# First product of a two-block kernel: input transposed without its norm, row factors applied to values, queries and keys

## The chip, the cores and the metric

One core of a Trainium2 chip runs the whole program. The metric is the device time of one execution in microseconds (us), the median of several runs. The trace is of one profiled execution.

## The reference, cut to what matters

Two transformer-like blocks on `x`, 256 rows of 1024, in fp32. The part at issue is the first layer of the first block:

```python
def rmsnorm(x, g):
    xf = x.astype(jnp.float32)
    y = xf * lax.rsqrt(jnp.mean(xf * xf, axis=-1, keepdims=True) + RMS_EPS)
    return (y * g.astype(jnp.float32)).astype(x.dtype)

hn = rmsnorm(h, norm_mix[layer])
# in chunked_band_attention(hn, ...), 16 heads of 64:
qkv = jnp.einsum('bsd,de->bse', h, w_qkv)
s = jnp.einsum('bqhd,bkhd->bhqk', q_c, k_band) * scale + bias
p = jax.nn.softmax(s, axis=-1)
o = jnp.einsum('bhqk,bkhd->bqhd', p, v_band)
```

After it come an output product, a squared-ReLU MLP, a gated recurrent layer with its MLP, and a second block with two SwiGLU products, windowed attention and pooling. The norm is a factor r for each row of x and a gain g for each of its 1024 features. A product of the normed row is r times the product of the row with its gains alone.

## The kernel before

**Numbers in two parts.** Every large product is made of three fp32r products: each operand is split into a high part (ACT copies it to fp32r) and a low part (DVE subtracts the high part), and TensorE adds high x high, low x high and high x low. Weights come from HBM in pieces of 128 x 1024 (512 KB) into four `raw` buffers, are split into `wh` (10 buffers) and `wl` (7 buffers), and a `raw` buffer is free again when its low part is made. `Core.load` and `Core.fetch` issue the DMAs on SP's queue, in the order of `c.plan`; `weights` asks for three pieces ahead.

**Order of the work.** TensorE runs its instructions in the order in which the program writes them. On the other engines a scheduler orders instructions by priority and readiness; `urgent()` raises the priority of a block, and `issue_after(ins)` keeps the instructions of a block behind `ins` on the engine that they share with it. Each engine then runs its queue in order.

**The start (`forward`).** The tiles `h[0]` and `h[1]` hold 128 rows of x each; `fetch(t)` loads one in two halves. `spread` loads the gain row of 1024 and, by two 1-row products with a column of ones, writes it to all 128 partitions in PSUM (line 230). `stat` squares a half row with its sum on ACT (line 488), `sum` adds the sums and the epsilon on DVE (497), `power` takes the power -1/2 on POOL (506), and `finish` multiplies h by r and by the gains on DVE into `hn` (512). `turned` transposes hn in eight blocks of 128 x 128 per tile on TensorE (527), and `split` makes from each four of them the two parts of `xt` (ACT line 109, DVE line 113). Tile 1 follows in the same way while the first product runs.

**The values (`a_gen`, name `v`).** The stationary operand is a block of xt, the moving one 512 columns of a weight. With `head=5` the first five of eight contraction blocks k are done for tile 0 and then for tile 1 (the high products of block k are written before the low ones of k-1); the transposes of tile 1 stand between the steps (`mid`). Then follow the rest, and the last three blocks per bank (`tail=3`), after which `evac_v` copies each bank to `vt`. 96 products of 512 columns in all, at lines 381 and 385 (a_v in the trace).

**Queries and keys (`b_gen`).** Four rounds of a query piece and a key piece, each of two blocks of 128 features. The weight is stationary, xt moves: the high parts with 512 columns (line 249), the low with 256 (258). `evac` calls `join`, which adds the two parts of a product: ACT copies one (337), DVE adds it to the other (341 for keys, 343 for queries, with the scale 1/8). During a round the attention of the heads of the round before is woven in: `scores` (734), softmax, `turn` (765), `apply` (776). `decay`, some thirty operations on 128 x 8 numbers for the recurrent layer, is written after the first round; its input `cols`, and for the second block `rope` and `sink`, are small DMAs on SP's queue.

Of the kernel before, what the change touches and what calls it, by code (L numbers as in the profile page):

```python
# [9 lines left out]
F32 = mybir.dt.float32  # L10
F32R = mybir.dt.float32r
AF = mybir.ActivationFunctionType
ALU = mybir.AluOpType
# [35 lines left out]
def run(gen):  # L49
    for _ in gen:  # L50
        pass
# [14 lines left out]
def rest():  # L66
    pass


class Core:  # L70
# [146 lines left out]
            self.nc.sync.dma_start(t, self.a["rows"][row : row + 1, :].to_broadcast([P, D]))  # L217
        return [t[:, n * 512 : (n + 1) * 512] for n in range(2)]

    def spread(self, row, name):  # L220

        nc = self.nc
        one = self.const.tile([1, P], F32, name="one")
        nc.vector.memset(one, 1.0)
        t = self.gb.tile([P, D], F32, tag="gb", name=f"row_{name}")
        nc.sync.dma_start(t[0:1, :], self.a["rows"][row : row + 1, :])
        out = []
        for n in range(2):
            out.append(self.psum(f"{name}_{n}"))
            nc.tensor.matmul(out[n], one, t[0:1, n * 512 : (n + 1) * 512], start=True, stop=True)  # L230
        return out

    def b_gen(self, xt, blocks, evac, fill=0, mid=(), late=(3, 4), whole=None):
# [129 lines left out]

        return lhs

    def a_gen(self, name, nk, lhs, evac, head=0, mid=(), tail=4, hook=(), late=0, half=False):


        nc = self.nc
        acc = {}

        def bank(t, n):
            if (t, n) not in acc:
                acc[t, n] = self.psum(f"a_{name}_{t}{n}")
            return acc[t, n]

        def high(k, t, n, part):
            w = self.weights(name, k)[:, n * 512 : (n + 1) * 512]  # L380
            nc.tensor.matmul(bank(t, n), lhs(k, t, part), w, start=k == 0 and not part, stop=False)  # L381

        def low(k, t, n):
            w = self.weights(name, k, True)[:, n * 512 : (n + 1) * 512]
            nc.tensor.matmul(bank(t, n), lhs(k, t, 0), w, start=False, stop=k == nk - 1)  # L385

        def mm(k, t, n):
            high(k, t, n, 0)
            high(k, t, n, 1)
            low(k, t, n)  # L390

        mid, hook = list(mid), list(hook)
        for t in range(2 if head else 0):
            for k in range(head):
                for part in range(2):
                    for n in range(2):
                        high(k, t, n, part)
                for n in range(2 if k else 0):
                    low(k - 1, t, n)
                if t == 0 and k >= head - 2 and mid:  # L400
                    mid.pop(0)()
                yield
            for n in range(2):
                low(head - 1, t, n)
        for f in mid:
            f()
        for k in range(head, nk - tail):
            for t in range(2):
                for n in range(2):
                    mm(k, t, n)  # L410
                yield
        normed = bool(hook)
        if normed:
            self.approach(name, nk - 1)
        for t in range(2):
            for n in range(2):
                for i, k in enumerate(range(nk - tail, nk)):
                    mm(k, t, n)
# [30 lines left out]
class Norm:  # L449


    def __init__(self, c, row, name, scale=None, spread=False):
        self.c, self.name, self.scale = c, name, scale
        self.g = (c.spread if spread else c.gain)(row, f"g_{name}")
        self.sums, self.hn = {}, {}
        self.x = None

# [59 lines left out]
    def turned(self, t):  # L517


        def half(n):  # L520
            c = self.c
            if self.x is None:

                self.x = c.xt.tile([P, KD, 2, 2, P], F32R, tag="xt", name=f"xt_{self.name}")
            ps = c.psum(f"tr_{self.name}{t}_{n}")
            for i in range(4):
                c.nc.tensor.transpose(
                    ps[:, i * P : (i + 1) * P], self.hn[t][:, n * 512 + i * P : n * 512 + (i + 1) * P],
                    c.ident,
                )  # L530
            k = slice(4 * n, 4 * n + 4)
            with c.urgent():
                c.turned = c.split(
                    self.x[:, k, t, 0, :], self.x[:, k, t, 1, :], ps.rearrange("p (k n) -> p k n", n=P)
                )

        return [lambda: half(0), lambda: half(1)]


class Norm2(Norm):  # L540
# [88 lines left out]
@with_exitstack  # L629
def forward(ctx: ExitStack, tc, a, out):  # L630
    nc = tc.nc
    c = Core(ctx, tc, a)
    ctx.enter_context(tc.manual_schedule(engines={mybir.EngineType.PE}))

    def fetch(t):
        for n in range(2):
            cc = slice(n * 512, (n + 1) * 512)
            nc.sync.dma_start(c.h[t][:, cc], a["x"][0, t * P : (t + 1) * P, cc])

    norm = Norm(c, R_MIX0, "mix0", spread=True)  # L640
    fetch(0)
    c.planned("v", a["w_v"])
    with c.urgent():
        for n in range(2):
            norm.stat(0, n)
        norm.finish(0)
    c.hold = True
    c.load(1)
    for i, f in enumerate(norm.turned(0)):
        f()  # L650
        with c.behind():
            if not i:
                c.lows()
            else:
                c.hold = False
            c.load(2 + i)
            if not i:
                fetch(1)
    with c.urgent(), c.behind():
        for n in range(2):  # L660
            norm.stat(1, n)
        norm.finish(1)
# [36 lines left out]

def attention(c, norm, cols):  # L700
# [3 lines left out]
    vt = c.slot("vt")  # L704

    def evac_v(t, n, ps, cc):
        nc.scalar.activation(vt[:, t * D + n * 512 : t * D + (n + 1) * 512], ps, AF.Copy)

    run(c.a_gen(
        "v", KD, lambda k, t, s: xt[:, k, t, s, :], evac_v, head=5, mid=norm.turned(1), tail=3,  # L710
    ))

    qt, kt, ot = c.slot("qt"), c.slot("kt"), c.slot("ot")
    bias = [c.slot(f"bias{i}") for i in range(2)]
# [3 lines left out]

    def evac(name, f, ps):
        dst = blk(qt if name[0] == "q" else kt, f)  # L720
        c.join(
            dst.rearrange("p (t n) -> p t n", n=P), ps, f"{name}_{f}", scale=0.125 if name[0] == "q" else 1.0
        )

    state = {}

# [69 lines left out]
    for j in range(4):  # L796
        gen = c.b_gen(xt, [(f"q{j}", 0, 2 * j), (f"k{j}", 0, 2 * j)], evac)
        weave(gen, 8, pairs(2 * j - 2, 2 * j) if j else [])
        if not j:
            nc.sync.dma_start(cols, a["cols"])  # L800
            decay(c, cols)
    norm = Norm(c, R_MLP0, "mlp0")
    gen = c.a_gen(
        "ao", KD, c.stationary("ao", lambda i: ot[:, i * 512 : (i + 1) * 512]), norm.evac,
# [163 lines left out]
def mixer(c, norm, cols):  # L968
    nc, a = c.nc, c.a
    xt = norm.x  # L970
    rope = c.const.tile([P, 2, 2, 16], F32, name="rope")
    nc.sync.dma_start(rope, a["rope"])
    sink = c.const.tile([P, 8], F32, name="sink")
    nc.sync.dma_start(sink, a["sink"][0:1, :].to_broadcast([P, 8]))
    less = c.const.tile([P, 8], F32, name="less")
    nc.vector.tensor_scalar_mul(less, sink, -1.0)
    pm, pools, mix, ro, rot = (c.slot(f"mix{i}") for i in range(5))
# [337 lines left out]
```

## Time and profile before

| | us |
|---|---|
| median of 3 runs (lowest, highest) | 1009.74 (1009.57, 1010.5) |
| the profiled execution | 1008.66 |
| its span in the trace | 1006.9 |
| TensorE busy | 994.7 (99%) |
| VectorE (DVE) busy | 665.7 (66%) |
| ScalarE (ACT) busy | 573.7 (57%) |
| GpSimd (POOL) busy | 28.8 (3%) |

The profile follows each instruction of every engine. PE is TensorE's products, PEld the loading of their stationary operands, which overlaps them, SP the queue that issues most DMAs. Ends of products are modelled, since they are pipelined: the step from one start to the next is the better measure of their rate. `[0.62 <-DVE kt L341]` behind a row says that the engine had been idle for 0.62 us and what ended that. A row in order of time merges neighbours (`x8`). Most fp32 products (not fp32r) appear as two records. Lines are those of the kernel before.

### The profile page before, as it was taken

What the parts mean: (1) busy time and instruction counts of PE and PEld (TensorE: products, weight loads), DVE (VectorE), ACT (ScalarE), POOL (GpSimd) and SP (SyncE); (2) the same over time, 40 slices, a digit from 0 to 9 for tenths busy, and PEclk for the clock granted to TensorE, in tenths of its full rate; (3) what the DMA queues carried; (4) which work ended last, traced back from release to release, by engine and by line L of the source; (5) the groups of instructions that cost most, each with busy time, mean ns of one, the idle gap of its engine ahead of it and who ended that gap; (6) DMA issues with size and microseconds to landing.
All of it is one profiled execution on the core that took longest, in us unless ns stands there. A gap on an engine that the chain in (4) does not pass through costs nothing.

```text
span 1006.9 us, 14600 instructions
## 1 busy us (share of the span) xinstructions
PE 994.7 (99%) x5558; PEld 856.5 (85%) x5558; DVE 665.7 (66%) x1070; ACT 573.7 (57%) x950; POOL 28.8 (3%) x49
## 2 busy tenths in 40 slices
PE   8999999999999999999999999999999999999997
PEld 6887898888889989888888988888888698888885
DVE  6677487676648768867555876565557767756553
ACT  6576556455537965654544665555436856555541
POOL 1000000000012200000000000000000000000000
PEclk9999999999999999999999999999999999999999
DMA  8944157667744454767653476676526428566641
GB/s 279 328 149 132 58 185 254 209 229 231 256 141 131 142 168 147 252 201 239 203 191 126 156 246 190 196 252 213 182 70 224 147 65 268 193 196 203 208 143 42
DMA packets 52055, 187.41 MB, mean 186 GB/s; under 512 B 6161, under 2 KB 6161, under 8 KB 51474
## 3 DMA queue, kind: packets, MB, share of 16 engines
q1 hardware_dynamic: 51986, 186.49, 56.8%
q8 instruction: 43, 0.70, 0.3%
q14 instruction: 26, 0.21, 0.1%
HBM read 185.42 MB, written 1.05 MB: 185 GB/s over the span
## 4 chain that ended last, share of the span: by engine, by line
PE 89%; ACT 4%; DMA 3%; DVE 2%; issue 1%; POOLq 0%; POOL 0%; SPq 0%; ACTq 0%; DVEq 0%
PE b_m L249 12%; PE a_n L381 11%; PE a_d L381 8%; PE b_g L249 8%; PE b_u L249 8%; PE b_m L258 6%; PE a_n L385 6%; PE b_g L258 4%; PE b_u L258 4%; PE a_d L385 4%; PE b_r L270 2%; PE a_v L381 2%; PE a_ao L381 1%; PE a_ro L381 1%; PE a_mo L381 1%; PE b_r L249 1%
## 5 line engine op out<-in xcount | busy, mean ns | idle before, releaser
L381 PE MATMUL a_n<-wh_n,l_n 128*128 128x512 f32 x512 | 157.9, 390 | 0.0
L249 PE MATMUL b_m<-xt_mlp,wh_m 128*128 128x512 f32 (+1 forms) x608 | 124.8, 357 | 0.0
L249 PEld LDWEIGHTS b_m<-xt_mlp,wh_m 128*128 128x128 f32 x608 | 100.6, 189 | 14.9
L381 PEld LDWEIGHTS a_n<-wh_n,l_n 128*128 128x128 f32 x512 | 95.7, 188 | 19.5
L113 DVE TENSOR_TENSOR wl_n<-raw_n,wh_n 128x1024 fp32r<-128x1024 f32 x64 | 78.1, 1223 | 51.5 <-PE a_n L385 38.8
L134 ACT ACTIVATE wh_n<-raw_n 128x1024 fp32r<-128x1024 f32 x64 | 67.9, 1061 | 76.2 <-DMA raw_n<-in_w_m_dram 75.3
L381 PE MATMUL a_d<-wh_d,l_d 128*128 128x512 f32 x352 | 108.7, 390 | 0.0
L385 PE MATMUL a_n<-wl_n,l_n 128*128 128x512 f32 x256 | 99.6, 389 | 0.0
L113 DVE TENSOR_TENSOR wl_m<-raw_m,wh_m 128x1024 fp32r<-128x1024 f32 x64 | 77.3, 1221 | 24.7 <-PE b_m L258 17.3
L134 ACT ACTIVATE wh_m<-raw_m 128x1024 fp32r<-128x1024 f32 x64 | 67.4, 1058 | 44.3 <-DMA raw_m<-in_w_m_dram 44.1
L249 PE MATMUL b_g<-xt_ffn,wh_g 128*128 128x512 f32 (+1 forms) x416 | 86.5, 359 | 0.2 <-ACT wh_g L134 0.2
L249 PE MATMUL b_u<-xt_ffn,wh_u 128*128 128x512 f32 (+1 forms) x384 | 85.0, 373 | 0.0
L249 PEld LDWEIGHTS b_g<-xt_ffn,wh_g 128*128 128x128 f32 x416 | 69.2, 189 | 11.2 <-ACT wh_g L134 0.4
L381 PEld LDWEIGHTS a_d<-wh_d,l_d 128*128 128x128 f32 x352 | 65.8, 188 | 13.5
L113 DVE TENSOR_TENSOR wl_d<-raw_d,wh_d 128x1024 fp32r<-128x1024 f32 x44 | 53.6, 1223 | 35.2 <-PE a_d L385 23.6
L249 PEld LDWEIGHTS b_u<-xt_ffn,wh_u 128*128 128x128 f32 x384 | 66.9, 189 | 11.4
L113 DVE TENSOR_TENSOR wl_g<-raw_g,wh_g 128x1024 fp32r<-128x1024 f32 x44 | 53.5, 1221 | 34.5 <-PE b_u L258 27.3
L134 ACT ACTIVATE wh_d<-raw_d 128x1024 fp32r<-128x1024 f32 x44 | 46.7, 1062 | 50.1 <-DMA raw_d<-in_w_d_dram 45.3
L385 PE MATMUL a_d<-wl_d,l_d 128*128 128x512 f32 x176 | 68.5, 389 | 0.0
L134 ACT ACTIVATE wh_u<-raw_u 128x1024 fp32r<-128x1024 f32 x44 | 46.4, 1058 | 38.1 <-DMA raw_u<-in_w_u_dram 38.0
L258 PEld LDWEIGHTS b_m<-xt_mlp,wl_m 128*128 128x128 f32 x512 | 65.6, 191 | 2.0
L258 PE MATMUL b_m<-xt_mlp,wl_m 128*128 128x256 f32 x512 | 67.1, 283 | 0.0
(253 smaller groups left out, 1744.1 us busy)
## 6 DMA issues: line engine op xcount, KB each, us to landing
raw_m<-in_w_m_dram SPq DMA_DIRECT2D x64, 512.0 KB, 4.3
raw_n<-in_w_m_dram SPq DMA_DIRECT2D x64, 512.0 KB, 3.7
raw_g<-in_w_g_dram SPq DMA_DIRECT2D x44, 512.0 KB, 4.4
raw_u<-in_w_u_dram SPq DMA_DIRECT2D x44, 512.0 KB, 3.5
raw_d<-in_w_d_dram SPq DMA_DIRECT2D x44, 512.0 KB, 4.2
raw_r<-in_w_ri_dram SPq DMA_DIRECT2D x16, 512.0 KB, 4.1
raw_v<-in_w_v_dram SPq DMA_DIRECT2D x8, 512.0 KB, 4.7
raw_q<-in_w_qk_dram SPq DMA_DIRECT2D x8, 512.0 KB, 4.7
```

Of the source, the lines that this page charges most:

```text
L113: return self.nc.vector.tensor_tensor(out=lo, in0=src, in1=hi.bitcast(F32), op=ALU.subtract).ins
L134: self.nc.scalar.activation(hi[:, :n], raw[:, :n], AF.Copy)
L249: nc.tensor.matmul(o, hi[:, kk, fb * P : (fb + 1) * P], x, start=k == 0 and t != 1, stop=False)
L258: nc.tensor.matmul(o, lo[:, kk, fb * P : (fb + 1) * P], xt[:, k, :, 0, :], start=False, stop=k == KD - 1)
L270: nc.tensor.matmul(ps, w[:, kk, fb * P : (fb + 1) * P], xt[:, k, :, part, :], start=k == 0 and w is hi and not part, stop=k == KD - 1 and ...
L381: nc.tensor.matmul(bank(t, n), lhs(k, t, part), w, start=k == 0 and not part, stop=False)
L385: nc.tensor.matmul(bank(t, n), lhs(k, t, 0), w, start=False, stop=k == nk - 1)
```

## The change

`First` takes the place of `Norm` for the first norm. The raw tiles of x are transposed; the gains, turned into a column for each of the eight feature blocks by eight products with one column, are applied when the transposed blocks are split (`high` on ACT, `low` on DVE, per 128 x 128 block, in a written order). The row factors are computed later, from the same squares. Values get them as the scale of `evac_v`; for queries and keys a product of a matrix of ones with a diagonal matrix writes the 256 factors along the free dimension on all partitions (`along`), and each joined block is multiplied by it, queries on POOL and keys on DVE. `idle(n)` issues n products of ones into a PSUM bank that nothing reads. The gain row and the first weight are loaded by ACT's queue, the rest by SP's. `spread`, the keyword `mid` as a list and the argument `spread` of `Norm` go; `mid` of `a_gen` becomes a table from (tile, block) to what is written there, and `head` is 4. The diff, cut to its core:

```diff
+class First(Norm):
+    def order(self, engine, f):
+        last = self.orders.get(engine)
+        with self.c.urgent():
+            with self.c.tc.issue_after(last) if last is not None else nullcontext():
+                self.orders[engine] = f().ins
+    def columns(self):
+        nc, ps = self.c.nc, self.c.psum(f"g_{self.name}")
+        one = self.c.const.tile([1, 1], F32, name="one")
+        nc.vector.memset(one, 1.0)
+        for k in range(KD):
+            nc.tensor.matmul(
+                ps[:, k : k + 1], self.row[0:1, k * P : (k + 1) * P], one, start=True, stop=True
+            )
+        self.order("DVE", lambda: nc.vector.tensor_copy(self.g, ps[:, 0:KD]))
+    def turn(self, t, n):
+        ps = self.banks[t, n] = self.c.psum(f"tr_{self.name}{t}_{n}")
+        for i in range(4):
+            cc = slice(n * 512 + i * P, n * 512 + (i + 1) * P)
+            self.c.nc.tensor.transpose(ps[:, i * P : (i + 1) * P], self.c.h[t][:, cc], self.c.ident)
+    def high(self, t, k):
+        ps = self.banks[t, k // 4][:, (k % 4) * P : (k % 4 + 1) * P]
+        self.order("ACT", lambda: self.c.nc.scalar.activation(
+            self.x[:, k, t, 0, :], ps, AF.Copy, scale=self.g[:, k : k + 1]
+        ))
+    def low(self, t, k):
+        ps = self.banks[t, k // 4][:, (k % 4) * P : (k % 4 + 1) * P]
+        self.order("DVE", lambda: self.c.nc.vector.scalar_tensor_tensor(
+            out=self.x[:, k, t, 1, :], in0=ps, scalar=self.g[:, k : k + 1],
+            in1=self.x[:, k, t, 0, :].bitcast(F32), op0=ALU.mult, op1=ALU.subtract,
+        ))
+    def means(self):
+        c = self.c
+        for t in range(2):
+            with c.tc.issue_after(self.orders["ACT"]):
+                for n in range(2):
+                    self.stat(t, n)
+            self.rows.append(self.power(self.sum(t), f"{self.name}{t}"))
+    def spread(self):
+        c, nc = self.c, self.c.nc
+        ps = c.psum(f"along_{self.name}")
+        for t in range(2):
+            cc = slice(t * P, (t + 1) * P)
+            nc.tensor.matmul(ps[:, cc], self.ones, self.diag[t], start=True, stop=True)
+        self.last = nc.scalar.activation(self.along, ps[:, 0:T], AF.Copy).ins
+    def diagonal(self):
+        nc, self.diag = self.c.nc, []
+        for t in range(2):
+            d = self.c.tmp.tile([P, T], F32, tag="e0", name=f"diag_{t}")[:, 0:P]
+            nc.vector.tensor_scalar_mul(d, self.c.ident, self.rows[t])
+            self.diag.append(d)
@@ forward
+    def feed(i, engine=nc.sync):
+        c.fed = engine.dma_start(raw[i], a["w_v"][i]).ins
+    nc.scalar.dma_start(norm.row[0:1, :], norm.from_row)
+    feed(0, nc.scalar)
     fetch(0)
+    for i in range(1, 4):
+        feed(i)
+    fetch(1)
...
+    def half(i):
+        norm.order("DVE", lambda: nc.vector.tensor_copy(hi[i][:, left], raw[i][:, left]))
+        norm.order("ACT", lambda: nc.scalar.activation(hi[i][:, right], raw[i][:, right], AF.Copy))
+    def rest(i):
+        norm.order("DVE", lambda: nc.vector.tensor_tensor(
+            out=lo[i], in0=raw[i], in1=hi[i].bitcast(F32), op=ALU.subtract
+        ))
+    norm.ones = ones = c.const.tile([P, P], F32, name="ones")
+    nc.vector.memset(ones, 1.0)
+    unused = c.psum("unused")
+    def idle(n):
+        for _ in range(n):
+            nc.tensor.matmul(unused[:, 0:P], ones, ones, start=True, stop=True)
+    idle(10)
+    norm.columns()
+    idle(10)
+    norm.turn(0, 0)
+    idle(3)
+    norm.high(0, 0)
+    half(0)
+    norm.low(0, 0)
+    for k in range(1, 4):
+        norm.high(0, k)
+        norm.low(0, k)
+    half(1)
+    rest(0)
+    rest(1)
+    for i in range(2, 4):
+        norm.order("ACT", lambda: nc.scalar.activation(hi[i], raw[i], AF.Copy))
+        rest(i)
@@ attention
-        nc.scalar.activation(vt[:, t * D + n * 512 : t * D + (n + 1) * 512], ps, AF.Copy)
+        nc.scalar.activation(
+            vt[:, t * D + n * 512 : t * D + (n + 1) * 512], ps, AF.Copy, scale=norm.rows[t]
+        )
+    def tile_1():
+        norm.turn(1, 0)
+        for k in range(4):
+            norm.high(1, k)
+            norm.low(1, k)
+        c.hold = False
+        with c.tc.issue_after(norm.orders["ACT"]):
+            c.load(6)
+    def others():
+        norm.turn(1, 1)
+        for t in range(2):
+            for k in range(4, 8):
+                norm.high(t, k)
+                norm.low(t, k)
+        norm.means()
+        norm.diagonal()
+    gen = c.a_gen(
+        "v", KD, lambda k, t, s: xt[:, k, t, s, :], evac_v, head=4, tail=3,
+        mid={(0, 0): lambda: norm.turn(0, 1), (0, 3): tile_1, (1, 1): others},
+    )
+    for step, _ in enumerate(gen):
+        if step == 16:
+            norm.spread()
...
-        c.join(
-            dst.rearrange("p (t n) -> p t n", n=P), ps, f"{name}_{f}", scale=0.125 if name[0] == "q" else 1.0
-        )
+        with c.urgent():
+            c.join(
+                dst.rearrange("p (t n) -> p t n", n=P), ps, f"{name}_{f}",
+                scale=0.125 if name[0] == "q" else 1.0,
+            )
+            engine = nc.gpsimd if name[0] == "q" else nc.vector
+            engine.tensor_tensor(out=dst, in0=dst, in1=norm.along, op=ALU.mult)
...
-            nc.sync.dma_start(cols, a["cols"])
-            decay(c, cols)
+            with c.tc.issue_after(c.fed):
+                nc.sync.dma_start(cols, a["cols"])
+            with c.tc.issue_after(norm.last):
+                decay(c, cols)
@@ mixer
-    nc.sync.dma_start(rope, a["rope"])
-    nc.sync.dma_start(sink, a["sink"][0:1, :].to_broadcast([P, 8]))
+    with c.tc.issue_after(c.fed):
+        nc.sync.dma_start(rope, a["rope"])
+        nc.sync.dma_start(sink, a["sink"][0:1, :].to_broadcast([P, 8]))
```

## Rows read from the trace of the kernel before

**Rows 1.** Page: the chain that ended last, share of the span by engine.

```profile
PE 89%; ACT 4%; DMA 3%; DVE 2%; issue 1%; POOLq 0%; POOL 0%; SPq 0%; ACTq 0%; DVEq 0%
```

**Rows 2.** Waits of TensorE, whole span: us in total, times, longest.

```profile
PE s L734 <- DVE kt L341: 0.8, 2, 0.6
```

**Rows 3.** Instructions in time order, 0 to 40 us: start, us, engine, line, operation.

```profile
0.85 0.17 DVE L224 MEMSET one<- 1x128 f32 x1
...
2.31 3.75 PE L230 MATMUL g_mix<-row_g_mix,one 1*128 1x512 f32 x4 [2.31 <-DMA row_g_mix<-in_rows_dram]
...
33.35 3.79 PE L249 MATMUL b_q<-xt_mix,wh_q 128*128 128x512 f32 x16
```

**Rows 4.** Chain that ended last, 0 to 70 us: start, us, what.

```profile
3.88 1.37 ACT hn_mix L488 x4
...
6.91 1.97 PE tr_mix L527 x8
8.87 3.62 PE a_v L381 x8
...
15.79 0.44 PE tr_mix L527 x4
...
18.54 1.83 PE a_v L381 x8
...
25.36 0.45 PE a_v L381 x2
25.81 0.23 PE a_v L385
```

**Rows 5.** Busy time by stretch: engines, TensorE's granted clock, DMA share, GB/s.

```profile
4.00:8.70 4.70, 3.85 (x11) 1.90 (x9) 1.58 (x4) 2.94 (x7) 0.55 (x1) 1.00 0.98 330
...
33.50:44.00 10.50, 10.50 (x62) 9.23 (x61) 6.03 (x7) 5.54 (x9) 1.04 (x2) 1.00 0.87 320
44.00:52.00 8.00, 8.00 (x54) 6.62 (x52) 5.55 (x14) 5.35 (x11) 0.00 (x0) 1.00 0.73 250
```

**Rows 6.** TensorE in time order, the second mixer's fp32 products, 773 to 784.

```profile
777.20 0.60 PE L1114 MATMUL py<-pdd,mix 128*128 128x256 f32 x2
777.64 1.05 PE L1104 MATMUL pd<-mix,mix 128*128 128x120 f32 x8
778.52 0.60 PE L1114 MATMUL py<-pdd,mix 128*128 128x256 f32 x2
```

**Rows 7.** Groups of instructions, 0 to 90 us: busy us, mean ns; idle.

```profile
L113 DVE TENSOR_TENSOR wl_v<-raw_v,wh_v 128x1024 fp32r<-128x1024 f32 x8 | 9.7, 1220 | 0.9 <-ACT wh_v L134 0.8
...
L343 DVE SCALAR_TENSOR_TENSOR qt<-b_q,tb_q 128x256 f32<-128x256 f32 x8 | 3.1, 415 | 1.9 <-ACT tb_q L337 1.9
...
L337 ACT ACTIVATE tb_q<-b_q 128x256 f32<-128x256 f32 x8 | 2.6, 375 | 0.0
...
L848 DVE TENSOR_SCALAR sp<-sp 128x8 f32<-128x8 f32 x9 | 1.5, 170 | 0.2
```

**Rows 8.** Instructions of line 882: ns min/median/max, first and last start.

```profile
L882 POOL TENSOR_TENSOR rec<-rec,rec x8: 726/953/1737, 319.4 to 337.6; 128x256 f32<-128x256 f32 x8
```

**Rows 9.** Instructions in time order, 58 to 61 us: a join, its scores.

```profile
58.91 0.42 DVE L341 TENSOR_TENSOR kt<-b_k,tb_k 128x256 f32<-128x256 f32 x1 [0.78 <-ACT tb_k L337]
...
60.28 0.92 PE L734 MATMUL s<-kt,qt 64*128 64x256 f32 x8
```

**Rows 10.** Instructions in time order, 71 to 79 us.

```profile
73.58 1.19 PE L258 MATMUL b_k<-xt_mix,wl_k 128*128 128x256 f32 x8
...
77.09 0.75 DVE L341 TENSOR_TENSOR kt<-b_k,tb_k 128x256 f32<-128x256 f32 x2
...
77.57 0.92 PE L734 MATMUL s<-kt,qt 64*128 64x256 f32 x8 [0.62 <-DVE kt L341]
```

**Rows 11.** Instructions in time order, 33 to 50 us: low parts, their use.

```profile
33.02 2.36 DVE L113 TENSOR_TENSOR wl_q<-raw_q,wh_q 128x1024 fp32r<-128x1024 f32 x2
...
49.06 2.17 PE L258 MATMUL b_q<-xt_mix,wl_q 128*128 128x256 f32 x16
```

More of the change, by code (lines that the diff above doesn't have):

```diff
@@ L218, in gain @@
         return [t[:, n * 512 : (n + 1) * 512] for n in range(2)]
[L220 to L231, printed above, removed]
     def b_gen(self, xt, blocks, evac, fill=0, mid=(), late=(3, 4), whole=None):
@@ L366, in stationary, with a_gen @@
         return lhs
-    def a_gen(self, name, nk, lhs, evac, head=0, mid=(), tail=4, hook=(), late=0, half=False):
+    def a_gen(self, name, nk, lhs, evac, head=0, mid=None, tail=4, hook=(), late=0, half=False):
         nc = self.nc
@@ L390, in mm @@
             low(k, t, n)
-        mid, hook = list(mid), list(hook)
+        mid, hook = mid or {}, list(hook)
         for t in range(2 if head else 0):
@@ L399, in a_gen @@
                     low(k - 1, t, n)
-                if t == 0 and k >= head - 2 and mid:
-                    mid.pop(0)()
+                if (t, k) in mid:
+                    mid.pop((t, k))()
                 yield
@@ L404, in a_gen @@
                 low(head - 1, t, n)
-        for f in mid:
-            f()
         for k in range(head, nk - tail):
@@ L449, with __init__ @@
 class Norm:
-    def __init__(self, c, row, name, scale=None, spread=False):
+    def __init__(self, c, row, name, scale=None):
         self.c, self.name, self.scale = c, name, scale
-        self.g = (c.spread if spread else c.gain)(row, f"g_{name}")
+        self.g = c.gain(row, f"g_{name}")
         self.sums, self.hn = {}, {}
@@ L537, in turned, with __init__ @@
         return [lambda: half(0), lambda: half(1)]
+class First(Norm):
+    def __init__(self, c, row, name):
+        self.c, self.name, self.scale = c, name, None
+        self.sums, self.hn, self.banks, self.rows = {}, {}, {}, []
+        self.x = c.xt.tile([P, KD, 2, 2, P], F32R, tag="xt", name=f"xt_{name}")
+        self.row = c.gb.tile([P, D], F32, tag="gb", name=f"row_{name}")
+        self.from_row = c.a["rows"][row : row + 1, :]
+        self.g = c.const.tile([P, KD], F32, name=f"g_{name}")
+        self.along = c.const.tile([P, T], F32, name=f"along_{name}")
+        self.orders = {}
+    def order(self, engine, f):
[48 more added lines that the diff above has]
+            self.diag.append(d)
@@ L638, in fetch @@
             nc.sync.dma_start(c.h[t][:, cc], a["x"][0, t * P : (t + 1) * P, cc])
-    norm = Norm(c, R_MIX0, "mix0", spread=True)
-    fetch(0)
[L642 to L646, printed above, removed]
-    c.hold = True
[L648 to L662, printed above, removed]
+    c.planned("v", a["w_v"])
+    norm = First(c, R_MIX0, "mix0")
+    raw, hi, lo = (
+        [pool.tile([P, 1024], dt, tag=tag, name=f"{tag}_v_{i}") for i in range(4)]
+        for pool, dt, tag in ((c.raw, F32, "raw"), (c.wh, F32R, "wh"), (c.wl, F32R, "wl"))
+    )
+    def feed(i, engine=nc.sync):
+        c.fed = engine.dma_start(raw[i], a["w_v"][i]).ins
+    nc.scalar.dma_start(norm.row[0:1, :], norm.from_row)
@@ new lines, in forward @@
+    feed(0, nc.scalar)
+    fetch(0)
+    for i in range(1, 4):
+        feed(i)
+    fetch(1)
+    c.loaded = c.fetched = 4
+    for i in range(4):
+        c.high["v", i], c.low["v", i] = hi[i], lo[i]
+    left, right = slice(0, 512), slice(512, 1024)
+    def half(i):
[5 more added lines that the diff above has]
+        ))
@@ L706, in evac_v @@
     def evac_v(t, n, ps, cc):
-        nc.scalar.activation(vt[:, t * D + n * 512 : t * D + (n + 1) * 512], ps, AF.Copy)
-    run(c.a_gen(
-        "v", KD, lambda k, t, s: xt[:, k, t, s, :], evac_v, head=5, mid=norm.turned(1), tail=3,
-    ))
+        nc.scalar.activation(
[24 more added lines that the diff above has]
+            norm.spread()
     qt, kt, ot = c.slot("qt"), c.slot("kt"), c.slot("ot")
@@ L720, in evac @@
         dst = blk(qt if name[0] == "q" else kt, f)
-        c.join(
-            dst.rearrange("p (t n) -> p t n", n=P), ps, f"{name}_{f}", scale=0.125 if name[0] == "q" else 1.0
-        )
+        with c.urgent():
+            c.join(
+                dst.rearrange("p (t n) -> p t n", n=P), ps, f"{name}_{f}",
+                scale=0.125 if name[0] == "q" else 1.0,
+            )
+            engine = nc.gpsimd if name[0] == "q" else nc.vector
+            engine.tensor_tensor(out=dst, in0=dst, in1=norm.along, op=ALU.mult)
     state = {}
```

## The prediction

> **What bounds the kernel now.** I read the page first: 89% of the chain that ended last runs on TensorE [rows 1]. The reader is to see that there is hardly a gap to close: a change pays only if TensorE does less, does it at a higher rate, or starts the dense work sooner. Of its waits after the first product starts, those that this change can touch are two of `s` on `kt`, 0.8 us together [rows 2]. So I next read the start in order of time [rows 3] and the chain through it [rows 4].
>
> The chain shows a start-up of 8.9 us before the first product of the values, a_v. Tile 0 of the input has landed when its squares begin at 3.88; square, power and scaling take until the transposes start at 6.91. And TensorE is slow when a_v begins: the first eight 512-column products take 3.62 us (0.45 each), later ones 1.83 for eight (0.23 each) [rows 4]. Eight transposes take 1.97 at first, four take 0.44 later (about 0.22 each by their issue, against 0.11). So the engine stands at the lower of its two levels (1.2 and 2.4 GHz) until about 12.5, although the granted clock of the page's rows is 1.00 there [rows 5]. The 1-row products of the gains from 2.31 to 6.06 and the transposes did not raise it; 3.6 us of a_v did. From 12.5 the stream is dense at the full rate, until q's first product at 33.35 [rows 3]. That instant, "V end", is my yardstick: what follows is the same work, so it shifts with it.
>
> **The change part by part.** All against the profiled execution (1008.66 us: its span 1006.9 and 1.76 around it).
>
> *Removed ahead of the transposes:* the norm of tile 0 (3.88 to 6.91, 3.0 us of the chain [rows 4]) and the two gain products (3.75 us, beside it) [rows 3]. Input can be transposed from about 4 us on.
>
> *Added ahead of the transposes, in TensorE's own order:* ten products of ones, eight gain columns, ten more products, four transposes. An fp32 product is two records. With 256 columns the two take 0.44 (777.20 to 777.64), so with 128 columns 0.22 at the full rate. Eight records, four of 120 columns and four of 16, take 0.88 (777.64 to 778.52), so one with hardly a column still takes about 0.11 [rows 6]. The columns: 16 records, between 0 (hidden behind their neighbours) and 16 x 0.22 = 3.5 (each as dear as a 256-column record); I take 16 x 0.11 = 1.8, the nearest row. Total 20 + 16 + 20 + 4 = 60 records x 0.11 = 6.6 us at the full level, 13.2 at the lower. They start once DVE has set the ones, about 1.2 by the memset at 0.85 [rows 3].
>
> The clock decides: if it rises at time R, the transposes end at T0 = 1.2 + 6.6 + (R - 1.2)/2 = 7.2 + R/2. Bounds: full at once 7.8, never 14.4. I take the nearest row, the 3.6 us that a_v spent at the lower level: R = 4.8, T0 = 9.6. So the 3 us freed from the norm are spent again: input that could be turned at 4 us is turned at 9.2, because the ones stand in front.
>
> *From T0 on, full rate:* three products of ones 0.66; 96 products of a_v at 0.227 (three of the tail take 0.45 + 0.23 = 0.68 [rows 4]) 21.76; twelve transposes inside the stream (eight before) x 0.11 = 1.32; two products that spread the factors, four records, 0.44. Waits: ACT and DVE now split in 128-column pieces in a fixed order. A piece on ACT is under 0.375 (that is 256 columns), on DVE under 0.415, a whole low part 1.22 [rows 7]. Following these orders, the left half of the second weight is ready about 0.2 after TensorE wants it, and the first weight's low part about 0.25 after; the rest keeps ahead. I take 0.45, bounds 0 and 1.5. Sum 24.63, so V end = 9.6 + 24.63 = 34.23, against 33.35: **+0.88**. All fast 32.43 (-0.92); R = 8 gives 35.83 (+2.5).
>
> *Weights by two queues:* I book nothing. The 16 engines were already busy 0.98 of the stretch 4.0 to 8.7 at 330 GB/s [rows 5]; input tile 0 and four weights are 2.6 MB, landed by about 10 us, the last of them wanted at T0 + 2.7. Uncovered (if T0 were 7) it would cost up to 1 us. The Trainium skill ("DMA: Bandwidth & Descriptors", Issuing engines are not separate DMA queues) says that issuing from several engines saves only issue time, since all run on the same 16 engines; by it the sum has 0 here as well, and a hope of earlier landing has no ground.
>
> *Values:* the factor rides in the evacuation that exists; free. Squares and powers of both tiles move behind the transposes; ACT and POOL have until the evacuation, by this count 5 us or more later; behind that cover they would cost what they are late.
>
> *Queries and keys:* eight multiplies on DVE (at most 0.42 each, a 128x256 row) and eight on POOL (0.73 to 1.74, the same shape) [rows 7, 8]. Per pair they lie between join and `scores`. Nearest use: `kt` joined 58.91 to 59.33, its product at 60.28 [rows 9], cover 0.95 for 0.42. Queries are joined several us earlier. If the cover went, 0.4 to 1.7 per late group. In sentences apart: the Trainium skill ("GPSIMD Engine Reference", Key points) says that POOL shares its SBUF interfaces with DVE and contends with DVE instructions of two SBUF inputs. The spread of the POOL row fits this; by it a query would come up to 1 us late, which its lead covers.
>
> *Joins made urgent:* scores(4) waits 0.62 because the joins stand behind weight splits: the low products of k end by 74.8, `kt` is joined at 77.09 [rows 10]. Put first, they end some 2 us sooner, and both waits on `kt` [rows 2] may go: -0.8 to 0; with the multiply added, I take **-0.6** (upper bound +0.4, one multiply uncovered).
>
> *Decay and small loads moved:* some 30 operations of 0.17 [rows 7], 5 us, go behind the spread, into 33.5 to 52, where DVE is free for 6.9 of 18.5 [rows 5]. Covered by the weights' lead: low parts made at 33.02 to 35.4 are first used at 49.06 [rows 11]. Without that cover up to 5 us; nothing is near it. The cols, rope and sink DMAs move later in SP's queue, behind the weights; nobody waits for them on the path. ACT issues two DMAs at the start, when it has only its table to load.
>
> Sum: +0.88 - 0.6 = **+0.3 us**. The profiled execution lies 1.08 below the median of the runs shown (1009.74); I put the change on the median: 1010.0.
>
> **The rivals.**
> *Faster.* The clock is up almost with the first products of ones, and the tiny columns hide. For: products follow one another from 1.2 on with no gap. Against: a_v, as dense, ran 3.6 us at the lower level. All fast -0.92, both `kt` waits gone -0.8, half the columns -0.9: -2.6, so 1007.1.
> *Slower.* The clock stays low through the ones and the columns: the columns are as thin as the gain products, after which the level was still low. Place: TensorE, 1.2 to T0. Price: half a microsecond for each one of delay. With R = 11, T0 = 12.7, V end 37.3, +4.0 - 0.6 = +3.4: 1013.1. It decides (slower by 2 us) from R = 8.2. For it: the lower level lasted to 12.5 before; against: ten dense products come first, at the lower level 4.4 us of them.
> *Late factors.* POOL beside DVE needs 1.7 or more, or joins hold DVE back, and three of the score groups wait some 1 us each on top of the forecast: 1013.0. Against: leads of several us for queries.
> *The transfer is hidden anyway:* taken as part of the forecast; the input waits for TensorE, not the reverse.
>
> **How the numbers follow.** Forecast 0.57 (its own range 1008.3 to 1011.8), faster rival 0.23, slower clock 0.14, late factors 0.06. A measurement here tells 0.2% (2.0 us) from no change: below 1007.7 comes the faster rival with most of its weight and a little of the forecast's lower end, 0.23; above 1011.8 the two slow ones, 0.19; between 0.58. Range: from the faster rival's centre 1007.1, a little below it for waits counted too high, to 1012.6, short of the slow clock's centre: 1006.9 to 1012.6.
>
> **What would show it.** TensorE in order of time: ones from about 1.2, at 0.44 a product, then 0.22 from near 4.8; columns about 1.8 us; first transposes at 9.2, first a_v near 10.3 at 0.23 each from the start; q's first product at 34.2. Waits on `kt` gone. Wrong if the transposes start before 7.5 (then input and weights bound it and I mis-sized the ones), if a_v still starts at 0.45, or if waits on `along`, `qt` or `kt` appear between 44 and 100.

## The result and the profile after

The changed kernel takes 1025.83 us (median of 4 runs, 1024.74 to 1027.18), the kernel before 1010.12 beside it (1009.57 to 1010.85): a ratio of 1.0154 [1.0143, 1.0166]. Forecast were 1010.0, next to no change (+0.3 us), and a range of 1006.9 to 1012.6. The kernel is slower by 15.7 us, far outside that range.

The profiled execution took 1025.92 us, with a span of 1024.1, 17.2 more than before. The yardstick divides it: q's first product (V end) stands at 48.75 instead of 33.35 [rows 3], which is +15.4; what follows takes 975.35 instead of 973.55, +1.8. So most of the loss is at the start, before the first product is done.

The page of the changed kernel, the chain that ended last by engine, hardly differs from [rows 1]. A share of 1000 us doesn't show a loss of 15:

```profile
PE 90%; ACT 5%; DVE 2%; DMA 2%; issue 1%; POOL 0%; POOLq 0%; DVEq 0%; ACTq 0%; SPq 0%
```

The waits of TensorE in the changed kernel (us in all, times, longest), beside [rows 2]:

```profile
PE along_mix L590 <- DVE diag L597: 4.1, 2, 2.2
PE s L859 <- DVE kt L848: 2.3, 2, 1.5
PE a_v L368 <- DVE wh_v L725: 1.3, 1, 1.3
```

The waits on `kt`, which should have gone, rose from 0.8 to 2.3; two waits of the spread on the diagonals are new. TensorE in order of time in the changed kernel (start, us), beside [rows 3, 4]:

```profile
1.08 4.64 PE L740 MATMUL unused<-ones 128*128 128x128 f32 x20 [1.08 <-DVE sp L972]
5.65 3.57 PE L552 MATMUL g_mix<-one,row_mix 1*128 1x1 f32 x16
9.15 4.64 PE L740 MATMUL unused<-ones 128*128 128x128 f32 x20
13.58 0.79 PE L561 MATMUL tr_mix<-ident,h 128*128 128x128 f32 x4
14.21 0.83 PE L740 MATMUL unused<-ones 128*128 128x128 f32 x6
14.83 1.49 PE L368 MATMUL a_v<-wh_v,xt_mix 128*128 128x512 f32 x4
...
48.75 3.79 PE L236 MATMUL b_q<-xt_mix,wh_q 128*128 128x512 f32 x16
```

The first forty records of ones take 0.23 each, the columns 0.22: that is the lower of TensorE's two levels (1.2 and 2.4 GHz) all the way. Only the last six records of ones stand closer, about 0.1 apart. The level rises near 14.0, not at 4.8, and the transposes end at 14.4 (forecast 9.6). The granted clock in the page's rows is 1.00 there, as it was at the start of the kernel before.

All engines of the changed kernel from 14.4 us, in order of time. The reader is to follow the blocks of 128 columns, which ACT and DVE hand to each other:

```profile
14.41 0.37 ACT L565 ACTIVATE xt_mix<-tr_mix,g_mix 128x128 fp32r<-128x128 f32 x1 [3.62 <-PE tr_mix L561]
14.67 0.62 ACT L726 ACTIVATE wh_v<-raw_v 128x512 fp32r<-128x512 f32 x1
...
15.20 0.37 ACT L565 ACTIVATE xt_mix<-tr_mix,g_mix 128x128 fp32r<-128x128 f32 x1
...
15.60 0.35 DVE L571 SCALAR_TENSOR_TENSOR xt_mix<-tr_mix,g_mix,xt_mix 128x128 fp32r<-128x128 f32 x1 [0.44 <-ACT xt_mix L565]
...
15.99 0.37 ACT L565 ACTIVATE xt_mix<-tr_mix,g_mix 128x128 fp32r<-128x128 f32 x1 [0.42 <-DVE xt_mix L571]
...
18.01 1.16 PE L368 MATMUL a_v<-wh_v,xt_mix 128*128 128x512 f32 x4 [1.26 <-DVE wh_v L725]
```

The copy of a block on ACT waits for the low part of the block before on DVE, and the other way round: 0.79 us from one high copy to the next, where ACT alone needs 0.37. The second weight's half (L725) stands behind four such blocks, and TensorE waits for it until 18.01. Further weights are split between blocks, so the last copy ends at 37.1, and behind it come the squares:

```profile
36.91 0.61 PE L368 MATMUL a_v<-wh_v,xt_mix 128*128 128x512 f32 x2
37.36 0.39 PE L372 MATMUL a_v<-wl_v,xt_mix 128*128 128x512 f32 x1
39.57 0.49 PE L590 MATMUL along_mix<-diag,ones 128*128 128x128 f32 x2 [1.82 <-DVE diag L597]
42.30 0.80 PE L590 MATMUL along_mix<-diag,ones 128*128 128x128 f32 x2 [2.25 <-DVE diag L597]
42.75 1.20 PE L368 MATMUL a_v<-wh_v,xt_mix 128*128 128x512 f32 x2
43.75 0.63 PE L372 MATMUL a_v<-wl_v,xt_mix 128*128 128x512 f32 x1
```

```profile
37.05 0.62 ACT L473 ACTIVATE hn_mix<-h 128x512 f32<-128x512 f32 x1
...
39.23 1.27 ACT L804 ACTIVATE vt<-a_v,r_mix 128x512 f32<-128x512 f32 x2 [0.25 <-POOL r_mix L491]
40.38 0.63 ACT L473 ACTIVATE hn_mix<-h 128x512 f32<-128x512 f32 x1
40.90 0.20 ACT L473 ACTIVATION_READ_ACCUMULATOR hn_mix<-h 128x1 f32 x1
```

(TensorE, then ACT, both in order of time.) The spread stands in TensorE's own order ahead of the last fifteen products; it needs the row factors, these need the squares, and the first square starts at 37.05, the last at 40.38. Ahead of the last one ACT copies two finished banks of the values (L804), which themselves wait for the first row factor: the fourth square starts 1.4 us after the third is done (38.98), and that is part of the second wait of 2.25. TensorE stands still for 4.1 us in all and then runs slowly. The stretches of the changed kernel (busy time by engine, granted clock, DMA share, GB/s), in the columns of [rows 5]:

```profile
10.50:19.00 8.50, 7.22 (x38) 6.17 (x37) 2.88 (x7) 4.04 (x9) 0.00 (x0) 1.00 0.01 4
19.00:37.75 18.75, 18.56 (x82) 14.25 (x81) 14.71 (x21) 11.77 (x23) 0.00 (x0) 1.00 0.76 252
37.75:42.75 5.00, 0.93 (x4) 0.75 (x5) 1.78 (x7) 4.75 (x11) 1.10 (x2) 0.85 0.82 261
42.75:48.00 5.25, 5.25 (x14) 4.11 (x14) 1.60 (x2) 3.21 (x5) 0.52 (x1) 0.50 0.96 381
```

From 42.75 to 48.0 the granted clock is 0.50, the lower level, after 5 us in which TensorE was busy for 0.93. The four groups of three products there take 5.27 us (42.75 to 48.02) instead of 4 x 0.68: 2.6 lost. The first row shows another thing: between 10.5 and 19 us the transfers rest (4 GB/s). The four raw buffers are full; the next transfer waits for the first low part of a weight, which VectorE starts at 17.78, and is issued at 19.07.

So the +9.7 us between the transposes and V end (34.4 us instead of 24.63) are 4.1 of waits of the spread, 2.6 of the lower level behind them, 1.3 of the second weight, less the 0.45 forecast; some 2 us are left, in small waits of TensorE and in the spread's own records at the lower level (0.45 for two, 42.30 to 42.75), and are not divided further.

### The profile page after: what moved, and what is told of

Same layout as the page of the kernel before. It is cut to its first block, busy times and chain, and to the rows that moved or that the text cites. A ratio compares the mean times of both kernels' runs of the same rounds, so it can differ in the third digit from the quotient of the medians.

```text
span 1024.1 us, 14782 instructions
## 1 busy us (share of the span) xinstructions
PE 1006.5 (98%) x5620; PEld 868.6 (85%) x5620; DVE 671.0 (66%) x1092; ACT 575.8 (56%) x963; POOL 37.0 (4%) x57
## 4 chain that ended last, share of the span: by engine, by line
PE 90%; ACT 5%; DVE 2%; DMA 2%; issue 1%; POOL 0%; POOLq 0%; DVEq 0%; ACTq 0%; SPq 0%
PE b_m L236 12%; PE a_n L368 11%; PE a_d L368 8%; PE b_g L236 8%; PE b_u L236 8%; PE b_m L245 6%; PE a_n L372 6%; PE b_g L245 4%; PE b_u L245 4%; PE a_d L372 4%; PE b_r L257 2%; PE a_ro L368 1%; PE a_ao L368 1%; PE b_q L236 1%; PE b_k L236 1%; PE a_mo L368 1%
## 5 line engine op out<-in xcount | busy, mean ns | idle before, releaser
L113 DVE TENSOR_TENSOR wl_u<-raw_u,wh_u 128x1024 fp32r<-128x1024 f32 x44 | 53.5, 1223 | 23.4 <-PE b_g L245 21.2
```

Source lines behind the costliest of these rows:

```text
L113: return self.nc.vector.tensor_tensor(out=lo, in0=src, in1=hi.bitcast(F32), op=ALU.subtract).ins
```

## Experiments

The first four each take away one suspect of the start: the ones, the squares' place, the turns of ACT and DVE, and the columns among the ones. Behind each expectation stand the median, its ratio to the kernel before run beside it with a 95% interval, and V end in the trace.

**1. No products of ones.**

```
-    idle(10)
     norm.columns()
-    idle(10)
     norm.turn(0, 0)
-    idle(3)
```

> The changed kernel without its 23 products of ones. Theory A (the ones are pure delay: they ran 4.6 + 4.6 us at the lower level before the first transposes): the columns then start when the gain row lands (about 2.4) and last 3.6 us at the lower level, ACT's table load (1.3 us) now lies on the path, first product of the values near 8.2 instead of 14.8; it starts at the lower level and gives back some 2 us. Waits on the factors stay. 1021 us. Rival B (the ones buy the clock and are worth their time): no gain or a loss, 1024 or more.

1021.27 us, ratio 1.011 [1.0092, 1.0127]; V end 41.77. The ones cost 4.6 us: the transposes start at 5.96, but the first a_v only at 8.79, since now the first weight is late (1.72). The waits of the spread stay (4.6), and so does the lower level behind them. V end is 7.0 earlier, but what follows it takes 976.8 instead of 975.35, for the waits on `kt` are 3.8 instead of 2.3.

**2. Squares early**, behind the second group of transposes, and the diagonals ahead of the last blocks.

```
         norm.turn(1, 0)
+        with c.urgent():
+            norm.means()
+        norm.orders["ACT"] = c.squared
...
         norm.turn(1, 1)
+        norm.diagonal()
```

> The changed kernel with the squares and powers of both tiles, and the diagonal, put ahead of the copies of tile 1 on ACT and DVE instead of behind all copies. Theory A: the two waits of the spreading products on the diagonal (4.1 us) go, and with them the stretch of 6 us at granted clock 0.50 that follows (3.3 us lost): 1018.5 us, no wait of along on diag, granted clock 1.00 from 38 to 50 us. Rival B (the squares only move the delay to the copies of tile 1, and the clock falls for another reason): 1023 or more.

1018.57 us, 1.0084 [1.0056, 1.0112]; V end 41.88. No wait for the spread is left, and the granted clock of the same stretch is 1.00 (the windows of this kernel):

```profile
34.00:42.00 8.00, 8.00 (x38) 6.50 (x37) 5.07 (x8) 5.97 (x10) 0.00 (x0) 1.00 0.98 356
42.00:48.00 6.00, 6.00 (x36) 5.29 (x35) 1.08 (x1) 2.17 (x4) 1.04 (x2) 1.00 1.01 408
```

V end gains 6.9, which is 4.1 + 2.6 read above, and 0.2: the lower level there came from the wait.

**3. Four highs, then four lows**, so that no block waits for the other engine's last one.

```
-        norm.high(0, k)
-        norm.low(0, k)
+        norm.high(0, k)
+    for k in range(4):
+        norm.low(0, k)
```

(and so for the other three groups)

> The changed kernel with the four copies on ACT written before the four subtractions on DVE, instead of in turn. Theory A (ACT waits for DVE between pieces only because of the order in which they are written, 0.79 us a piece): the wait of 1.3 us at 16.8 goes, weight splits no longer get between the pieces, the squares come some 5 us earlier, and most of the wait on the diagonal and of the low clock behind it goes: 1019 us. Rival B (two engines cannot read one PSUM bank in step, so nothing changes): 1025 us.

1020.0 us, 1.009 [1.0064, 1.0115]; V end 41.09. ACT now copies three blocks in 0.88 (this kernel in order of time):

```profile
15.02 0.88 ACT L565 ACTIVATE xt_mix<-tr_mix,g_mix 128x128 fp32r<-128x128 f32 x3
15.77 0.64 ACT L726 ACTIVATE wh_v<-raw_v 128x512 fp32r<-128x512 f32 x1
```

The squares come earlier with the copies, and the wait of the spread is gone here too. So 2 and 3 remove the same loss by two ways, and their gains cannot add in full. In both traces what follows V end takes 977.7 or more, some 2.4 above the changed kernel: behind one wait on `kt` (2.5 and 2.3) the granted clock is 0.70 from 70 to 74.

**4. Twenty products of ones together**, then the columns.

```
-    idle(10)
+    idle(20)
     norm.columns()
-    idle(10)
```

> The changed kernel with the twenty products of ones in one run, and the columns after them. Theory A (products of ones do raise the clock, but the columns between the two runs broke them up): the clock rises within the ones, between 4.6 and 8 us, the transposes end at about 10.5 instead of 14.4: 1022 us. Rival B (such products never raise it): the ones stay at 0.23 a record throughout, the level rises only with the transposes or values: 1025.8 us.

1023.1 us, 1.0127 [1.0103, 1.0151]; V end 45.57. Both kernels run nothing but ones up to 5 us. Windows of one microsecond, first this kernel (records in brackets behind TensorE's busy time):

```profile
4.00:5.00 1.00, 1.00 (x11) 1.00 (x10) 0.00 (x0) 0.00 (x0) 0.00 (x0) 1.00 1.02 395
...
10.00:11.00 1.00, 0.39 (x4) 0.20 (x2) 0.00 (x0) 0.99 (x3) 0.00 (x0) 0.99 0.16 62
11.00:12.00 1.00, 0.87 (x2) 0.64 (x3) 0.45 (x2) 0.87 (x3) 0.00 (x0) 0.50 0.07 27
```

then the changed kernel:

```profile
4.00:5.00 1.00, 1.00 (x7) 1.00 (x6) 0.00 (x0) 0.00 (x0) 0.00 (x0) 1.00 1.05 404
11.00:12.00 1.00, 1.00 (x7) 1.00 (x6) 0.00 (x0) 0.00 (x0) 0.00 (x0) 1.00 0.06 23
14.00:15.00 1.00, 1.00 (x11) 1.00 (x9) 0.19 (x1) 0.59 (x2) 0.00 (x0) 1.00 0.00 0
```

Kept together, the ones run at 11 records in the fifth microsecond; with the columns among them, at 6 or 7 until 14. Experiment 4 so shows that the place of the columns decides when the level rises, not by what means: the rates differ before the first column starts. The early rise is then thrown away: TensorE idles between 10 and 11 for the first copies, and the granted clock is 0.50 when a_v begins.

**5. The three together** (1, 2 and 3).

> The changed kernel with three edits together: no products of ones, squares and powers ahead of the copies of tile 1, four copies before four subtractions. Theory A (three separate causes): the gains add up as far as they are not the same, 1021.3 of the run without ones less 7 for the wait on the diagonal and the low clock behind it, less 0.5: 1013.8 us, q's first product near 34. Rival B (they share one cause): no better than the best alone, 1018.

1014.2 us, 1.0045 [1.003, 1.006]; V end 35.31, span 1011.7. Of the 17.2 us in the span 12.4 are gone. What is left against before is V end +2.0 and the waits on `kt` (3.6 instead of 0.8, +2.8).

**6. The same without the factors on q and k** (the multiplication is left out).

```
-            engine = nc.gpsimd if name[0] == "q" else nc.vector
-            engine.tensor_tensor(out=dst, in0=dst, in1=norm.along, op=ALU.mult)
```

> As e5_three, with the multiplies of queries and keys by the row factors left out (the scores are then of unscaled queries and keys). Theory A (the multiply of a key stands behind a weight's low part in DVE's order, and TensorE waits 2 to 4 us on kt in all): 1010.5 us, waits of s on kt under 1 us. Rival B (DVE is late there because of the decay and of late low parts, not of the multiplies): within 1 us of e5_three.

1011.51 us, 1.0017 [1.0007, 1.0028]; wait on `kt` 0.3. The multiplication costs 2.7. The traces agree: what follows V end falls from 976.4 to 973.9, where the kernel before has 973.55. (V end itself is 37.0 in this trace, since the first weight came late.)

**7. The decay as early as before** (not held behind the spread).

```
-            with c.tc.issue_after(norm.last):
-                decay(c, cols)
+            decay(c, cols)
```

> As e5_three, with the decay and its small DMA not held behind the spread, as in the kernel before. Theory A (multiplies): within 0.7 us of e5_three. Rival B (some 30 operations of 0.17 us on DVE between 48 and 72 us make the keys late): 2 us faster, waits of s on kt under 1.5 us.

1016.11 us (1012.31 to 1018.76), 1.0046 [1.003, 1.0063], waits on `kt` 4.3 in the traced run. This is not settled. The traced run is the longest of seven: behind a wait of 3.6 its granted clock is 0.63 from 66 to 70. Four runs had a mean granted clock of 0.996 or 0.997 and took 1016.1 to 1018.8; the three with 0.998 took 1012.3 to 1012.8, some 1.6 less than such runs of kernel 5 (1013.8 to 1014.2). That is near rival B's 2 us, yet in the trace the long wait stands with no piece of the decay around it, behind a low part and a multiplication.

**8. Table loaded early, first weight behind tile 0 on the other queue.**

```
-    feed(0, nc.scalar)
+    with c.urgent():
+        c.prime(AF.Copy)
     fetch(0)
-    for i in range(1, 4):
+    for i in range(4):
```

> As e5_three, with ACT's table loaded at once by a copy of one column, and the first weight on SP's queue behind tile 0 instead of on ACT's queue beside it. Theory A (the table load, 1.3 us, waits for the gains and lies on the path; and on its own queue the first weight shares the engines with three others and lands at 8.2): first product of the values at 7.0 instead of 8.8, 1012 us. Rival B (the columns, done at 6.0, and the pieces on ACT and DVE bound it anyway): less than 0.7 us from e5_three.

1014.32 us, 1.0045 [1.0029, 1.0061]. B's number held. The table load starts at 1.29, but the first weight's halves start at 8.01 and a_v at 8.58. With ACT's queue they started at 6.52 in kernel 5 and at 8.22 in kernel 1: the spread within one queue is as large as the step between the two. The run changes table and queue together, so it doesn't test the second queue alone: a gain from the table may hide a loss from the later weight. The Trainium skill ("DMA: Bandwidth & Descriptors", Issuing engines are not separate DMA queues) says that transfers issued by several engines run interleaved on the same 16 DMA engines; no run here shows otherwise, and none isolates it (6.52 and 8.22 from ACT's queue, 8.01 from SP's).

**9. The keys' multiplication on GpSimd too.**

```
-            engine = nc.gpsimd if name[0] == "q" else nc.vector
+            engine = nc.gpsimd
```

> The kernel with the three edits of the start (no products of ones, squares early, four highs ahead of four lows), and the keys' multiplication by the row factors moved from VectorE to GpSimd, where the queries' already is. Theory A, the keys' wait is the multiplication's place in VectorE's order (behind the low part of a weight, 1.22 us): waits of the scores on kt 3.6 -> about 1.5 us, 1014.2 -> about 1012 us. Rival B, the price is the second operation itself: GpSimd takes 0.74 to 1.73 us for one, where VectorE takes 0.48, so the waits stay at 3.6 us or grow and the time is 1014 us or more.

1017.14 us, 1.0061 [1.0043, 1.0078]. B: the waits grow (the waits of TensorE in this kernel, then a stretch with its granted clock in the third column from the end):

```profile
PE s L860 <- POOL kt L849: 4.7, 3, 3.2
```

```profile
66.00:70.00 4.00, 3.50 (x14) 2.75 (x15) 3.77 (x15) 2.25 (x7) 2.19 (x2) 0.65 0.69 190
```

The waits grew by 1.1 from kernel 5, the stretch behind V end by 2.6. The rest is the lower level behind the wait of 3.2: 0.65 from 66 to 70 and 0.93 from 70 to 74 lose 1.7 (an estimate, 4 x 0.35 + 4 x 0.07). The only run of this kernel with a mean granted clock of 0.998 took 1014.33, so most of the step from 1014.2 is that level. The queries' lead hides GpSimd's duration; the keys have none.

**10. The gain fetched as columns**, a 128x8 input of its own; the 16 column products and their copy go.

```
-    nc.scalar.dma_start(norm.row[0:1, :], norm.from_row)
+    nc.scalar.dma_start(norm.g, a["gain0"])
...
-    norm.columns()
```

> The three edits, and the gain of the first norm fetched as 128x8 columns by a transfer of its own (a relaid input), so that the 16 products of one column (2.5 to 6.0 us) and the copy behind them go. Theory A, what is left of the start's loss is the late first pieces: the transposes then stand at about 4.3 us instead of 6.0, the table is loaded before them, and the first product of the values waits for the first weight alone (landed 6.3): first a_v 8.1 -> about 7.0, end of the values 35.3 -> 34.2, 1014.2 -> about 1013.1 us. Rival B, the lower clock level at the start takes it back (fewer products before the values, so the rise comes as many us after the first product as now): end of the values within 0.4 of 35.3, 1014 us.

1011.94 us, 1.0018 [1.0007, 1.0029]; first a_v 6.45, V end 33.12. A held, with twice the gain expected at V end (2.2 for 1.1).

**11. The same with unbroken ones**, 12 ahead of the first transposes and 10 behind them.

> The kernel with the gain as fetched columns, with 12 products of ones before the first transposes (1.1 to about 3.9 us) and 10 behind them, now with no products of one column among them. Theory A, the clock: unbroken, they bring the rise to about 5 to 6 us, in front of the values, whose first 4 us then run at the upper level: about 2 us less than without them, 1011 us. Rival B, they hold up the transposes and the first product as much as they give: within 0.7 us of the kernel without them.

1011.93 us, 1.0008 [0.9997, 1.0019]. V end 32.73, and a_v runs at the upper level from its start (TensorE in order of time):

```profile
1.08 4.30 PE L729 MATMUL unused<-ones 128*128 128x128 f32 x24 [1.08 <-DVE sp L963]
5.23 0.60 PE L550 MATMUL tr_mix<-ident,h 128*128 128x128 f32 x4
5.66 2.40 PE L729 MATMUL unused<-ones 128*128 128x128 f32 x20
7.82 1.18 PE L368 MATMUL a_v<-wh_v,xt_mix 128*128 128x512 f32 x4
```

B, by its number: the ones hold up a_v by 1.4 us (7.82 against 6.45) and give 1.8 back, 0.4 at V end; the medians don't differ. Yet V end is now ahead of the kernel before (33.35), by 0.6. The start is repaired; the waits on `kt` (2.3) aren't.

**12. The keys' join and multiplication in halves**: join, join, multiply, multiply.

```
+                for t, cc in enumerate(cuts):
+                    nc.vector.tensor_tensor(out=dst[:, cc], in0=ps[:, t, 0, :], in1=tb[:, t, :], op=ALU.add)
+                for cc in cuts:
+                    nc.vector.tensor_tensor(out=dst[:, cc], in0=dst[:, cc], in1=norm.along[:, cc], op=ALU.mult)
```

> The kernel with the gain fetched as columns and unbroken products of ones, and each key's join and multiplication on VectorE done in two halves of 128 columns: join, join, multiply, multiply, so that no low part of a weight (1.22 us) stands between a join and its multiplication. Theory A, the place in VectorE's order makes the waits of the scores on kt (2.3 us): they fall to about 0.9, and the time to about 1010.5 us, level with the kernel before the change. Rival B, the second operation itself does (two more halves, some 0.2 us a group, and the keys' join is late anyway): waits stay within 0.5 of 2.3 us, 1011.9 us.

1010.7 us, 1.0007 [0.9996, 1.0017]. By its waits B, one of 1.9 instead of three of 2.3; by its time A. The two don't belong together: the traced run is one of four of twelve with a mean granted clock of 0.996 or 0.997 (1011.2 to 1013.5), the other eight took 1009.6 to 1010.9. No low part stands between join and multiplication any more, but one stands ahead of both at the wait (this kernel, in order of time, then the stretch behind it):

```profile
59.56 0.17 DVE L971 TENSOR_SCALAR sp<-sp 128x8 f32<-128x8 f32 x1
59.64 1.22 DVE L113 TENSOR_TENSOR wl_q<-raw_q,wh_q 128x1024 fp32r<-128x1024 f32 x1
60.78 0.48 DVE L842 TENSOR_TENSOR kt<-b_k,tb_k 128x128 f32<-128x128 f32 x2
61.18 0.48 DVE L844 TENSOR_TENSOR kt<-kt,along_mix 128x128 f32<-128x128 f32 x2
...
61.81 1.12 PE L855 MATMUL s<-kt,qt 64*128 64x256 f32 x8 [1.92 <-DVE kt L844]
```

```profile
62.00:66.00 4.00, 4.00 (x16) 3.09 (x14) 3.72 (x20) 2.57 (x7) 0.00 (x0) 0.57 0.64 192
```

VectorE makes four pieces of the decay (58.96 to 59.73) and then a low part, with the keys' join queued behind them. So the place in VectorE's order is part of the wait, and more than the one place that I named. The wait costs more than its 1.9: the granted clock of 0.57 behind it loses another 1.7 (an estimate, 4 x 0.43). Neither 11 nor 12 can be told from the kernel before, and none of the twelve beats it.

## Why the prediction was wrong

*The level of the clock* (the step R = 4.8). The sum around it was right: by T0 = 7.2 + R/2, with the measured R of 14.0, T0 is 14.2; the transposes ended at 14.4, and the columns cost what was booked for the lower level (3.57 for 16 records). What failed is the value of R. I took the nearest row, 3.6 us of a_v, and let the columns count as work like any other, although the same prediction said that thin products had not raised the level before. Experiment 4 shows that the columns' place makes the difference (in the fifth microsecond the level is up when they come behind all the ones); how they do it isn't shown. The slower rival had this mechanism and this place, but its example, R = 11, gives 1013.1, and R = 14 would give 1014.6. It is a third of the miss at V end: 14.5 us (48.75 against 34.23) are 4.8 here and 9.7 in the next steps.

*The stalls behind T0* (0.45, bounds 0 and 1.5). This and the next step are the larger miss, 9.7 us. I compared durations of single pieces with TensorE's pace and didn't follow the order in which ACT and DVE wait for each other (0.79 a block, not 0.37), nor what else is put between the blocks. Experiment 3 takes these turns away and gains 5.8 us; the waits of the spread go with them.

*"ACT and POOL have until the evacuation."* The cover was named wrongly. The reader of the row factors that counts isn't the evacuation but the spread, for it stands in TensorE's order, where everything behind it waits too. That is 4.1 of waiting and 2.6 of the lower level; experiment 2 takes both away. The prediction named waits on `along` as a sign of being wrong, but for 44 to 100 us; they stand at 39.57 and 42.30. That TensorE would run at the lower level after standing still (0.50 from 42.75 to 48.0) was in none of its terms.

*-0.6 on `kt`.* It became +1.5 (2.3 instead of 0.8). The order on VectorE in the changed kernel, beside [rows 10]:

```profile
75.23 0.42 DVE L328 TENSOR_TENSOR kt<-b_k,tb_k 128x256 f32<-128x256 f32 x1 [0.37 <-ACT tb_k L324]
75.57 1.22 DVE L113 TENSOR_TENSOR wl_q<-raw_q,wh_q 128x1024 fp32r<-128x1024 f32 x1
76.70 0.42 DVE L848 TENSOR_TENSOR kt<-kt,along_mix 128x256 f32<-128x256 f32 x1
```

The join is urgent, yet its multiplication comes behind a low part of 1.22 us. My cover of 0.95 for 0.42 held for a multiplication directly behind its join. Without it (experiment 6) the wait is 0.3, about what I expected of the urgent joins alone.

*The weights' lead as cover for the decay.* The transfers rested from 10.5 to 19 us, so the lead was less than I counted on. That its loss is what puts low parts between join and multiplication is not shown: in 11 and 12 the start is early again, and waits of 1.9 to 2.3 stay. What the decay's place costs stays open with experiment 7.

*Right:* no wait for queries on GpSimd appears; the rest after V end moves with it in the changed kernel, but for `kt` (1.5 of the 1.8). No run shows a gain from two queues, but none tests it alone.

## What to carry to other kernels

When work is taken out of a chain and spread over two engines in small pieces, write down the order on each engine with the waits between them, and ask for every new value which instruction in the bounding engine's own queue reads it first. Products that only keep TensorE at work raised the level early where no thin ones were among them; where the real work followed without a gap they gave 0.4 us at V end and nothing that the median shows (experiment 11), and in the changed kernel they were delay (4.6 us, experiment 1). A second operation behind a join is as late as what the scheduler may put between the two. A wait of TensorE can cost more than its length: look at the granted clock of the stretch behind it, and at the mean granted clock of every run before a traced one is compared with a median.

## What was not expected of the hardware

The records of TensorE ran at half rate for 13 us (0.23 a record) while the granted clock of the rows was 1.00; behind a wait in mid-kernel the same column did show 0.50 (42.75 to 48.0). At the start it has to be read from the records' pace.

Ones alone reached the upper level in the fifth microsecond in kernels 4, 11 and 12, whose first columns came late or never. In the changed kernel, and in kernels 2 and 3, which start in the same way, the ones were still at 7 records in that microsecond, though the first column stands at 5.65 in the changed kernel's trace, after it. Why the difference shows ahead of the columns is open.

The lower level behind a wait doesn't follow the wait's length. It came behind 0.74 us (kernel 4, first a_v) and behind waits on `kt` of 1.9, 2.3, 2.5, 3.2 and 3.6 (kernels 12, 3, 2, 9, 7); behind 2.3, 2.3 and 2.0 (kernels 5, 8, 1) the granted clock stayed at 1.00. What decides between them is open. Where it came in the attention it lost some 1.7 us each time, an estimate from the granted clock over 4 or 8 us.
